# Experts with their third products inside the next expert's first one, and a second input projection begun during the first output projection

## The chip, the cores and the metric

The kernel runs on one core of one Trainium2 chip. The core has five engines with instruction queues of their own, which run in order: TensorE (PE, with its weight loads shown as PEld), VectorE (DVE), ScalarE (ACT), GpSimd (POOL) and SyncE (SP), on which most DMAs are issued. They wait for one another by semaphores. The metric is the device time of one execution in microseconds.

## The reference

Two model blocks stand one after the other, with 2,048 tokens of 1,024 columns. The first is a layer with attention and a Fourier branch. The second has latent attention beside a gated recurrence (mLSTM), then a mixture of experts, then a gated embedding and a last norm. All in 32-bit floats; where a product needs the precision, the kernel splits a factor into a rounded high part and a low remainder (`hi`, `lo`) and adds three products. The parts that the change touches:

```python
# end of the first block
h = h + jnp.einsum('ble,ed->bld', mixed, w_out[i]); h = rmsnorm(h, final_g)
# second block: input projection
h = _rmsnorm(x, norm_mix_g[i])
c_q, c_kv, k_r, x_m, z, i_pre, f_pre = _split_in(h @ w_in[i])
q = (_rmsnorm(c_q, q_norm_g[i]) @ w_uq[i]).reshape(B, S, MLA_HEADS, NOPE_D + ROPE_D)
kv = (_rmsnorm(c_kv, kv_norm_g[i]) @ w_ukv[i]).reshape(B, S, MLA_HEADS, NOPE_D + V_D)
q_rope, k_rope = _apply_rope(q[..., NOPE_D:], cos, sin), _apply_rope(k_r, cos, sin)
...
# 32 experts, each token goes to two of them
def expert(args):
    xb, e = args
    return (jax.nn.silu(xb @ w_g[e]) * (xb @ w_u[e])) @ w_d[e]
```

## The kernel before

The program is a chain of phases. `phase_d` is the first output projection: 16 tiles of 128 tokens, three products of 512 columns for each pair of factors. `phase_e` is the second input projection, in eight groups of 256 tokens: `prep` reads a group's rows, norms them, transposes them on PE (L878) and splits them into `uhi` and `ulo`; a product with 424 columns of the weights (`th`, `tl`) gives the latents and gates, then one with 1,024 columns (`fh`, `fl`). These weights are read from memory and split on ACT and DVE (L76, L77) at the phase's start. `phase_f` makes queries, keys and values of the latents in four groups of 512 tokens: for each group it loads the rope tables (`cs`, `kr`), and three results (keys, queries, values) pass through a staging tile `o` with two buffers, copied by ACT and DVE in turn (`put`, L1081 and L1083) and stored from SP.

`phase_k` walks over the 32 experts; a step is called a block here. An expert has one tile of up to 128 tokens and, where more tokens came to it, a second one of 64 (`second`; here 16 of the 32, experts 0 to 6, 16, 17, 19, 21 to 25 and 28). In block x PE runs, in this order: two transposes of `sg`, the last expert's gated hidden rows (`out_a`, L2115); for a second tile `hidden2` (L2095, L2096); the first and second products of expert x (`hidden`, eight k steps of three products into `g`, with transposes of the next expert's rows between them, L2061, L2076, and of the second tile's `t` after the seventh step, L2136); `out_b`, the third products of expert x−1 into `py`; and `out2_b`, those of the second tile. Beside that the next weights are split: `raw` to `gh` on ACT and `gl` on DVE, `KW` = 2 slices of 256 columns (512) at a time, and `sd` to `dh` on ACT and `dl` on POOL, 512 columns at a time; DVE and ACT also do `sg` (L2090, L2091), the second tile's `t` (L2105, L2106, L2108, L2109), the splits of transposed rows (`xl`, `al`, `a`) and the copies of `py` to `y` (L2130, L2149). POOL gathers the rows of a later expert (L2049) and adds results to memory (L2052). All these helpers are L73 (ACT) and L74 (the other engine) of `split`. The tile framework sets the order on each engine and the waits; the two forms of a block stand in the two branches of an If.

Of the kernel before, what the change touches and what calls it, by code (L numbers as in the profile page):

```python
# [792 lines left out]
def phase_d(e):  # L793
# [5 lines left out]
    def post(wk, sm, pt, gb):  # L799
        def run(t, r, y):  # L800
            if t == 16:
                return
# [10 lines left out]

def phase_e(e, then):

# [10 lines left out]
    with ExitStack() as st:  # L826
# [3 lines left out]
        ut = pool("e_ut", 2)  # L830
        wk = pool("e_wk", 2)
        wt = pool("e_wt", 1)
        sm = pool("e_sm", 4)
        wp = pool("e_w", 1)
        pt = pool("e_pt", 2, space=PSUM)
        pm = pool("e_pm", 3, space=PSUM)
# [14 lines left out]
        fh, fl = load_split(e, wp, ld, w_in, 1024, 1024, "f", gcol, 416)  # L851
# [3 lines left out]
        taps = cst.tile([128, 4, 5], F32, name="taps")  # L855
        for k in range(4):
            nc.sync.dma_start(taps[:, :, k], d["conv_w_2"][0, k].rearrange("(h p) -> p h", p=128))
        nc.sync.dma_start(taps[:, :, 4], d["conv_b_2"][0].rearrange("(h p) -> p h", p=128))
        xms = [cst.tile([128, 4, 3 + GB], F32, name=f"xm{i}") for i in range(2)]
        nc.gpsimd.memset(xms[0][:, :, :3], 0.0)  # L860

        def prep(g):
            hi = ut.tile([128, 8, GB], F32R, name="uhi")
            lo = ut.tile([128, 8, GB], F32R, name="ulo")
            for i in range(GB // 128):
# [4 lines left out]
                junk = wk.tile([128, D], BF, name="junk", bufs=1)  # L870
# [11 lines left out]
        prep(0)  # L882
        pend = []
# [16 lines left out]
        for g in range(NG):  # L900
# [5 lines left out]
            for i in range(GB // 128):  # L906
# [6 lines left out]
                junk = wk.tile([128, D], BF, name="junk", bufs=1)  # L913
# [80 lines left out]
def phase_f(e, then):  # L994
# [16 lines left out]
    with ExitStack() as st:  # L1011
# [38 lines left out]
        yield  # L1050
        gates(e, pool)
        xp.append(pool("f_x1", 1))
        ld = pool("f_ld", 2)
        wk = pool("f_wk", 2)
        ps = pool("f_ps", 6, space=PSUM)
        e.stage = ld
        for g in range(S // GB):
            c = slice(g * GB, (g + 1) * GB)
            cs = ld.tile([128, 2, GB], F32, name="cs")
            for i, T in enumerate((CT, ST)):  # L1060
                nc.sync.dma_start(cs[:, i, :], bass.AP(tensor=T.tensor, offset=T.offset + g * GB, ap=[[0, 4], [S, 32], [1, GB]]))
            kr = ld.tile([64, GB], F32, name="kr")
            nc.sync.dma_start(kr, KRW[:, c])
# [7 lines left out]
            nc.sync.dma_start(KRT[:, c], ko[:, 0])  # L1071
# [7 lines left out]
            def put(o, p, i):  # L1079
                if i % 2:  # L1080
                    nc.scalar.activation(o, p, AF.Copy)  # L1081
                else:
                    nc.vector.tensor_copy(o, p)  # L1083
# [13 lines left out]
            nc.sync.dma_start(rows(QRT), r)  # L1097
            e.beside(then)
# [884 lines left out]
KW = 2  # L1983


def phase_k(e, last):
# [11 lines left out]
    with ExitStack() as st:  # L1998
# [13 lines left out]
        py = pool("k_py", 3, space=PSUM)  # L2012
# [26 lines left out]
        def split_down(w, s, x):  # L2039
            for k in range(2):  # L2040
                for i in range(2):
                    c = slice(i * 512, (i + 1) * 512)
                    split(e, w[0][:, k, c], w[1][:, k, c], s[:, 2 * k + i], eng=nc.gpsimd)
                    if k == i == 1 and x < 32:
                        load_down(x, s)
                    yield
# [37 lines left out]
        def hidden(w, x, sg, beside=lambda k: None):  # L2084

            g = pg.tile([128, 512], F32, name="g1")
# [33 lines left out]
        def out_b(w, a, dst):  # L2120
            y = op.tile([128, D], F32, name="y")
            for j in range(2):
                yp = py.tile([128, 512], F32, name="py")
                c = slice(j * 512, (j + 1) * 512)
                for k in range(2):
                    mm3(e, yp, (a[0][:, k], a[1][:, k]), (w[0][:, k, c], w[1][:, k, c]), k == 0, k == 1)
# [100 lines left out]
        def block(x, second):  # L2227
# [4 lines left out]
            if x:  # L2232
                a = out_a(SG[x - 1])
            parts(2)
            if second:
                sg2 = hidden2(W[x % 2], x2, x % 2)
                parts(2)
            a2 = []

            def beside(k):  # L2240
# [4 lines left out]
                if k == OUT2 and second:  # L2245
                    a2.append(out2_a(sg2))
# [4 lines left out]
                parts(1)  # L2251

            hidden(W[x % 2], X[x], SG[x], beside)
            if x:
                out_b(WD[(x - 1) % 2], a, e.dst[:, 0, x - 1:x])
            parts(16)
            if x < 31:
                all_of(split_down(WD[y], RD[y], x + 3))
            if second:
                out2_b(WD[x % 2], a2[0], e.dst[0:64, 1, x:x + 1])  # L2260
# [17 lines left out]
TURN, OUT2, TURN2 = (0, 2), 6, (4, 5)  # L2278
# [111 lines left out]
def body(e):  # L2390
    tc = e.tc
    with tc.tile_pool(name="consts", bufs=1) as cp:
# [9 lines left out]
        for _ in phase_d(e):  # L2402
            pass
# [52 lines left out]
```

## Time and profile before

| | us |
|---|---|
| runs (three) | 3589.45, 3594.97, 3596.04; median 3594.97 |
| profiled execution | 3607.51 |
| its span, mean granted clock | 3605.8, 0.966 |
| PE, PEld busy | 3364.2 (93%), 2611.3 (72%) |
| DVE, ACT, POOL busy | 2448.4 (68%), 2052.4 (57%), 696.2 (19%) |
| read from and written to memory | 333.81 MB, 135.24 MB |

The profiled execution is some 12.5 us longer than the median of the runs. By the trace `phase_d` runs from about 1357 us of the span to 1537, `phase_e` to 1827, `phase_f` to 1931, and the experts from 2892 to about 3380. A share of busy time is a mean over stages with different limits, so the stages are read one by one.

### The profile page before, as it was taken

What the parts mean: (1) busy time and instruction counts of PE and PEld (TensorE: products, weight loads), DVE (VectorE), ACT (ScalarE), POOL (GpSimd) and SP (SyncE); (2) the same over time, 40 slices, a digit from 0 to 9 for tenths busy, and PEclk for the clock granted to TensorE, in tenths of its full rate; (3) what the DMA queues carried; (4) which work ended last, traced back from release to release, by engine and by line L of the source; (5) the groups of instructions that cost most, each with busy time, mean ns of one, the idle gap of its engine ahead of it and who ended that gap; (6) DMA issues with size and microseconds to landing.
All of it is one profiled execution on the core that took longest, in us unless ns stands there. A gap on an engine that the chain in (4) does not pass through costs nothing. (4 is left out here: it accounts for less than half of the span.)

```text
span 3605.8 us, 48799 instructions
## 1 busy us (share of the span) xinstructions
PE 3364.2 (93%) x16556; PEld 2611.3 (72%) x16557; DVE 2448.4 (68%) x4612; ACT 2052.4 (57%) x3660; POOL 696.2 (19%) x729
## 2 busy tenths in 40 slices
PE   8999999999999999989986889989999989899798
PEld 6787766666666657789975667777788766677587
DVE  5835667888888854464365777877856568878554
ACT  4442357887777872253223777877833367677433
POOL 0000000000000010000032333332200046665332
PEclk9999999999999999999997999999999989899899
DMA  5333322111112035353247433322355678888753
GB/s 157 102 121 101 97 70 72 46 31 50 43 32 57 11 91 179 121 153 109 74 148 173 93 77 74 81 69 59 88 174 157 222 260 305 319 301 307 256 189 132
DMA packets 313432, 468.82 MB, mean 130 GB/s; under 512 B 66263, under 2 KB 201192, under 8 KB 304864
## 3 DMA queue, kind: packets, MB, share of 16 engines
q1 hardware_dynamic: 293622, 404.26, 36.9%
q0 software_dynamic: 19520, 60.97, 4.6%
q8 instruction: 148, 2.42, 0.3%
q14 instruction: 142, 1.16, 0.1%
HBM read 333.81 MB, written 135.24 MB: 130 GB/s over the span
## 5 line engine op out<-in xcount | busy, mean ns | idle before, releaser
L588 DVE TENSOR_TENSOR pl<-pe,ph 128x1024 fp32r<-128x1024 f32 (+1 forms) x272 | 340.6, 1253 | 89.0 <-ACT ph L581 87.7
L519 DVE TENSOR_REDUCE mx<-pmx 128x1 f32<-128x512 f32 x512 | 344.2, 684 | 82.9 <-PE pmx L518 76.5
L579 ACT ACTIVATE pe<-ps 128x1024 f32<-128x1024 f32 (+1 forms) x272 | 278.5, 1025 | 146.2 <-PE ps L577 135.9
L581 ACT ACTIVATE ph<-pe 128x1024 fp32r<-128x1024 f32 (+1 forms) x272 | 287.4, 1058 | 7.4
L74 DVE TENSOR_TENSOR gl<-raw,gh 128x512 fp32r<-128x512 f32 x256 | 235.2, 960 | 15.0 <-ACT gh L73 12.6
L576 PE MATMUL ps<-t,kh 128*128 128x512 f32 (+1 forms) x544 | 239.0, 439 | 0.5 <-ACT pe L579 0.5
L1280 DVE TENSOR_TENSOR pl<-pe,ph 128x512 fp32r<-128x512 f32 (+1 forms) x320 | 210.7, 662 | 40.5 <-ACT ph L1273 38.0
L577 PE MATMUL ps<-t,kl 65*128 65x512 f32 (+1 forms) x544 | 222.3, 409 | 0.0
L602 PE MATMUL acc<-ph,vh 128*65 128x512 f32 (+1 forms) x544 | 217.1, 399 | 0.0
L604 PE MATMUL acc<-pl,vh 128*65 128x512 f32 (+1 forms) x544 | 214.9, 395 | 0.0
L603 PE MATMUL acc<-ph,vl 128*65 128x512 f32 (+1 forms) x544 | 214.7, 395 | 0.0
L518 PE MATMUL pmx<-kh,t 128*128 128x512 f32 x512 | 207.1, 410 | 1.9 <-DVE mx L519 1.1
L1244 DVE TENSOR_REDUCE mx<-pmx 128x1 f32<-128x512 f32 (+2 forms) x320 | 190.7, 598 | 13.0 <-PE pmx L1243 12.6
L1271 ACT ACTIVATE pe<-ps 128x512 f32<-128x512 f32 (+1 forms) x320 | 166.9, 524 | 43.5 <-PE ps L1269 40.5
L74 POOL TENSOR_TENSOR dl<-sd,dh 128x512 fp32r<-128x512 f32 x128 | 172.8, 1371 | 71.6 <-ACT dh L73 69.2
L1273 ACT ACTIVATE ph<-pe 128x512 fp32r<-128x512 f32 (+1 forms) x320 | 179.5, 564 | 6.5
L1267 PE MATMUL ps<-t,kh 113*128 113x512 f32 (+1 forms) x320 | 138.0, 431 | 38.8 <-ACT pe L1271 29.8
L73 ACT ACTIVATE gh<-raw 128x512 fp32r<-128x512 f32 x256 | 143.4, 625 | 12.4 <-PE p L85 9.4
L83 PE MATMUL pm<-uhi,fh 128*128 128x256 f32 x512 | 145.3, 285 | 3.7 <-ACT fh L76 2.0
L84 PE MATMUL pm<-ulo,fh 128*128 128x256 f32 x512 | 143.6, 282 | 0.0
L85 PE MATMUL pm<-uhi,fl 128*128 128x256 f32 x512 | 143.2, 283 | 0.3 <-DVE fl L77 0.3
L788 DVE TENSOR_TENSOR y<-p,xt 128x1024 f32<-128x1024 f32 x32 | 39.2, 1224 | 152.9 <-PE p L85 151.2
(539 smaller groups left out, 9672.9 us busy)
## 6 DMA issues: line engine op xcount, KB each, us to landing
raw<-in_w_gate_e SPq DMA_DIRECT2D x32, 1024.0 KB
raw<-in_w_up_e SPq DMA_DIRECT2D x32, 1024.0 KB
sd<-in_w_down_e SPq DMA_DIRECT2D x32, 1024.0 KB
ws<-in_w_in SPq DMA_DIRECT2D x80, 256.0 KB
xt<-in_x SPq DMA_DIRECT2D x32, 512.0 KB
scr_X<-y SPq DMA_DIRECT2D x32, 512.0 KB
xt<-scr_X SPq DMA_DIRECT2D x32, 512.0 KB
yy<-scr_Y POOLq DMA_DIRECT2D x32, 512.0 KB, 5.0
```

Of the source, the lines that this page charges most:

```text
L74: (eng or nc.vector).tensor_tensor(lo, src, f32(hi), op=ALU.subtract)
L518: nc.tensor.matmul(p, t1[:, i * 128:(i + 1) * 128], kh[:, j * 512:(j + 1) * 512], start=True, stop=True)
L519: nc.vector.reduce_max(mx[:, i, j:j + 1], p, axis=AX.X)
L576: nc.tensor.matmul(p[:n, c], kh[:, k0:k0 + n], t1[:, c], start=True, stop=False)
L577: nc.tensor.matmul(p[:n, c], kl[:, k0:k0 + n], t2[:, c], start=False, stop=True)
L579: nc.scalar.activation(pe[:n], p[:n], AF.Exp, scale=0.125)
L581: nc.scalar.activation(ph[:n], pe[:n], AF.Copy)
L588: nc.vector.tensor_tensor(pl[:n], pe[:n], f32(ph[:n]), op=ALU.subtract)
L602: nc.tensor.matmul(A[u][j], vh[:n, i, :65], ph[:n, c], start=i == 0, stop=False)
L603: nc.tensor.matmul(A[u][j], vl[:n, i, :65], ph[:n, c], start=False, stop=False)
L604: nc.tensor.matmul(A[u][j], vh[:n, i, :65], pl[:n, c], start=False, stop=i == 16)
L1280: nc.vector.tensor_tensor(pl[:, c0:], pe[:, c0:], f32(ph[:, c0:]), op=ALU.subtract)
```

## The change

- `phase_e` begins inside `phase_d`: its constants, the 424 columns of weights, and group 0's rows are made beside `phase_d`'s last tiles (`NEXT`); the 1,024 columns and the rest come after it. Group buffers lie in two pools for that.
- `phase_f` reads the rope tables once, whole (18 DMAs), ahead of `gates`, and not per group; three staging buffers in place of two; of four copies out of PSUM ACT does three and DVE one, where each did two; the store of `ko` stands behind that of `r`.
- In the experts the third products (`out_b`, `out2_b`) stand after the sixth of the eight k steps of the next `hidden`, and their transposes after the fourth; `out_b` does its four products with `ah` ahead of its two with `al`. `g` has two PSUM buffers, `py` two in place of three. `KW` is 4, so that `gh` and `gl` are made 1,024 columns at a time; so are `dh` and `dl`.

The core of the diff:

```diff
-def phase_d(e):
+def phase_d(e, then):
...
     def post(wk, sm, pt, gb):
         def run(t, r, y):
+            if t == NEXT:
+                e.beside(then)
             if t == 16:
...
+NEXT = 13
...
 def phase_e(e, then):
...
-        ut = pool("e_ut", 2)
-        wk = pool("e_wk", 2)
+        ut = [pool("e_u0", 1)]
         wt = pool("e_wt", 1)
         sm = pool("e_sm", 4)
-        wp = pool("e_w", 1)
         pt = pool("e_pt", 2, space=PSUM)
-        pm = pool("e_pm", 3, space=PSUM)
...
             split(e, th[:, k], tl[:, k], ws[:, :NT], gcol[:, k:k + 1])
-        fh, fl = load_split(e, wp, ld, w_in, 1024, 1024, "f", gcol, 416)
...
         def prep(g):
-            hi = ut.tile([128, 8, GB], F32R, name="uhi")
-            lo = ut.tile([128, 8, GB], F32R, name="ulo")
+            hi = ut[g % 2].tile([128, 8, GB], F32R, name="uhi")
+            lo = ut[g % 2].tile([128, 8, GB], F32R, name="ulo")
...
         prep(0)
+        yield
+        wp = pool("e_w", 1)
+        ut.append(pool("e_u1", 1))
+        wk = pool("e_wk", 2)
+        pm = pool("e_pm", 3, space=PSUM)
+        fh, fl = load_split(e, wp, ld, w_in, 1024, 1024, "f", gcol, 416)
+        taps = wp.tile([128, 4, 5], F32, name="taps")
...
         yield
+        wt = pool("f_t", 1)
+        cst = wt.tile([128, 2, S], F32, name="cst")
+        krw = wt.tile([64, S], F32, name="krw")
+        for c in (slice(0, GB), slice(GB, S)):
+            for r in range(4):
+                for i, T in enumerate((CT, ST)):
+                    nc.sync.dma_start(cst[r * 32:(r + 1) * 32, i, c], T[:, c])
+            nc.sync.dma_start(krw[:, c], KRW[:, c])
         gates(e, pool)
         xp.append(pool("f_x1", 1))
         ld = pool("f_ld", 2)
-        wk = pool("f_wk", 2)
+        wk = pool("f_wk", 3)
         ps = pool("f_ps", 6, space=PSUM)
         e.stage = ld
         for g in range(S // GB):
             c = slice(g * GB, (g + 1) * GB)
-            cs = ld.tile([128, 2, GB], F32, name="cs")
-            for i, T in enumerate((CT, ST)):
-                nc.sync.dma_start(cs[:, i, :], bass.AP(tensor=T.tensor, offset=T.offset + g * GB, ap=[[0, 4], [S, 32], [1, GB]]))
-            kr = ld.tile([64, GB], F32, name="kr")
-            nc.sync.dma_start(kr, KRW[:, c])
+            cs, kr = cst[:, :, c], krw[:, c]
             xh, xl = X.pop(g)
...
@@ -1068,7 +1082,6 @@
             nc.gpsimd.tensor_tensor(ko[:, 0], kr[0:32], cs[0:32, 0], op=ALU.mult)
             nc.vector.tensor_mul(ko[:, 1], kr[32:64], cs[32:64, 1])
             nc.gpsimd.tensor_tensor(ko[:, 0], ko[:, 0], ko[:, 1], op=ALU.add)
-            nc.sync.dma_start(KRT[:, c], ko[:, 0])
...
             def put(o, p, i):
-                if i % 2:
+                if i:
                     nc.scalar.activation(o, p, AF.Copy)
                 else:
                     nc.vector.tensor_copy(o, p)
...
             nc.sync.dma_start(rows(QRT), r)
+            nc.sync.dma_start(KRT[:, c], ko[:, 0])
             e.beside(then)
             o = wk.tile([128, 4, GB], F32, name="o")
...
-KW = 2
+KW = 4
...
-        py = pool("k_py", 3, space=PSUM)
+        py = pool("k_py", 2, space=PSUM)
...
         def split_down(w, s, x):
             for k in range(2):
-                for i in range(2):
-                    c = slice(i * 512, (i + 1) * 512)
-                    split(e, w[0][:, k, c], w[1][:, k, c], s[:, 2 * k + i], eng=nc.gpsimd)
-                    if k == i == 1 and x < 32:
-                        load_down(x, s)
-                    yield
+                raw = s[:, 2 * k:2 * k + 2].rearrange("p a c -> p (a c)")
+                split(e, w[0][:, k], w[1][:, k], raw, eng=nc.gpsimd)
+                if k == 1 and x < 32:
+                    load_down(x, s)
+                yield
...
-            g = pg.tile([128, 512], F32, name="g1")
+            g = pg.tile([128, 512], F32, name="g1", bufs=2)
             for k in range(8):
...
             for j in range(2):
                 yp = py.tile([128, 512], F32, name="py")
                 c = slice(j * 512, (j + 1) * 512)
-                for k in range(2):
-                    mm3(e, yp, (a[0][:, k], a[1][:, k]), (w[0][:, k, c], w[1][:, k, c]), k == 0, k == 1)
+                terms = [(0, k, h) for k in range(2) for h in range(2)] + [(1, k, 0) for k in range(2)]
+                for n, (q, k, h) in enumerate(terms):
+                    nc.tensor.matmul(yp, a[q][:, k], w[h][:, k, c], start=n == 0, stop=n == 5)
...
             y = (x + 1) % 2
             steps = split_in(W[y], RG[y], x + 3) if x < 31 else iter(())
             parts = lambda n: [next(steps, None) for _ in range(n)]
-            if x:
-                a = out_a(SG[x - 1])
-            parts(2)
+            parts(1)
             if second:
                 sg2 = hidden2(W[x % 2], x2, x % 2)
-                parts(2)
-            a2 = []
+                parts(1)
+            a, a2 = [], []
             def beside(k):
                 if k in TURN and x < 31:
                     turn1(XR[(x + 1) % 2], X[x + 1], (TURN.index(k),))
                     if k == TURN[1]:
                         rows(x + 3)
-                if k == OUT2 and second:
-                    a2.append(out2_a(sg2))
                 if k in TURN2 and x % 2 == 1 and x < 31:
                     turn2(xr2, x2, (TURN2.index(k),))
                     if k == TURN2[1]:
                         rows2(x // 2 + 2)
-                parts(1)
+                if k == OUT and x:
+                    a.extend(out_a(SG[x - 1]))
+                if k == OUT and second:
+                    a2.append(out2_a(sg2))
+                if k == MID:
+                    if x:
+                        out_b(WD[(x - 1) % 2], a, e.dst[:, 0, x - 1:x])
+                    if second:
+                        out2_b(WD[x % 2], a2[0], e.dst[0:64, 1, x:x + 1])
+                if k % 2:
+                    parts(1)
             hidden(W[x % 2], X[x], SG[x], beside)
-            if x:
-                out_b(WD[(x - 1) % 2], a, e.dst[:, 0, x - 1:x])
-            parts(16)
+            parts(8)
             if x < 31:
                 all_of(split_down(WD[y], RD[y], x + 3))
-            if second:
-                out2_b(WD[x % 2], a2[0], e.dst[0:64, 1, x:x + 1])
             if x == 31:
                 out_b(WD[x % 2], out_a(SG[x]), e.dst[:, 0, x:x + 1])
...
-TURN, OUT2, TURN2 = (0, 2), 6, (4, 5)
+OUT, MID, TURN, TURN2 = 3, 5, (0, 2), (1, 4)
...
         e.flip()
         for _ in attention:
             pass
-        for _ in phase_d(e):
-            pass
-        e.flip()
         with ExitStack() as st:
             route = phase_j(e, st)
             first = embed(e, range(0, LATE), "right")
             out = phase_i(e, route, first)
             latent = phase_g(e, out)
             heads = phase_f(e, latent)
-            phase_e(e, heads)
+            second = phase_e(e, heads)
+            for _ in phase_d(e, second):
+                pass
+            e.flip()
+            for _ in second:
+                pass
             for rest in (heads, latent, out):
```

How the order moves is shown at three places. POOL, one block with a second tile (`dl` are the low parts of the down weights, the two L2052 or L2065 the additions of the first and of the second tile's result to memory). Before:

```order
L2049 DMA xr_28504<-scr_HF,tok 128x1024
L74 TENSOR_TENSOR dl_28449<-sd_28451,dh_28448 128x512 x3
L2052 DMA scr_Y<-y,dst 4096x1024
L74 TENSOR_TENSOR dl_28449<-sd_28451,dh_28448 128x512
L2052 DMA scr_Y<-y_30535,dst 4096x1024
```

Now:

```order
L2062 DMA xr_28500<-scr_HF,tok 128x1024
L2065 DMA scr_Y<-y,dst 4096x1024
L74 TENSOR_TENSOR dl_28457<-sd_28459,dh_28456 128x1024 x2
L2065 DMA scr_Y<-y_30362,dst 4096x1024
```

Three of four pieces of `dl` stood ahead of the addition of `y`; now both pieces, twice as wide, stand behind it.

DVE, one block with a second tile (`gl` are the low parts of the gate and up weights, `t` the second tile's gated rows, `xl` and `al` low parts of transposed rows). Before:

```order
L74 TENSOR_TENSOR gl_28445<-raw_28429,gh_28444 128x2x256
L74 TENSOR_TENSOR al<-pt,ah 128x256
L74 TENSOR_TENSOR gl_28445<-raw_28429,gh_28444 128x2x256 x6
L2106 TENSOR_TENSOR t_34775<-t_34775,g_34758 64x512
L74 TENSOR_TENSOR gl_28445<-raw_28429,gh_28444 128x2x256
L2109 TENSOR_TENSOR t_34775<-t_34775 64x256
L74 TENSOR_TENSOR xl<-pt,xh 128x512 x2
L74 TENSOR_TENSOR a_34834<-pt,a_34834 128x2x64
L2091 TENSOR_TENSOR sg<-sg,g_34785 128x256
L2130 COPY y<-py 128x512
L2149 TENSOR_TENSOR y_34871<-y_34871,py 64x512 x2
```

Now (a block that also has the row transposes of an odd expert, `x`):

```order
L74 TENSOR_TENSOR gl_28451<-raw_28433,gh_28450 128x4x256 x4
L2119 TENSOR_TENSOR t_34960<-t_34960,g_34943 64x512
L74 TENSOR_TENSOR xl<-pt,xh 128x512
L2122 TENSOR_TENSOR t_34960<-t_34960 64x256
L74 TENSOR_TENSOR x_28498<-pt,x_28498 128x8x64
L74 TENSOR_TENSOR xl<-pt,xh 128x512
L74 TENSOR_TENSOR al<-pt,ah 128x256
L74 TENSOR_TENSOR a_35015<-pt,a_35015 128x2x64
L74 TENSOR_TENSOR x_28498<-pt,x_28498 128x8x64
L2145 COPY y<-py 128x512
L2164 TENSOR_TENSOR y_35055<-y_35055,py 64x512 x2
L2104 TENSOR_TENSOR sg<-sg,g_34968 128x256
```

All four `gl` now stand ahead of `t`, and `sg` behind the copies of `y`.

ACT, from `phase_d`'s last norms on (L805 or L807 is the norm of a tile of `phase_d`, L871 or L868 that of a tile of `phase_e`). Before:

```order
L871 ACTIVATE junk,ss<-xt 128x1024 x2
L805 ACTIVATE junk,ss<-y 128x1024
L73 ACTIVATE uhi<-pt 128x4x128
L102 ACTIVATE rs_r<-ss 128x1
L73 ACTIVATE uhi<-pt 128x4x128 x3
L871 ACTIVATE junk,ss<-xt 128x1024
L76 ACTIVATE th<-ws,gcol 128x424 x3
L871 ACTIVATE junk,ss<-xt 128x1024
```

Now:

```order
L807 ACTIVATE junk,ss<-y 128x1024
L102 ACTIVATE rs_r<-ss 128x1
L73 ACTIVATE uhi<-pt 128x4x128 x2
L807 ACTIVATE junk,ss<-y 128x1024
L73 ACTIVATE uhi<-pt 128x4x128
L102 ACTIVATE rs_r<-ss 128x1
L73 ACTIVATE uhi<-pt 128x4x128
L76 ACTIVATE fh<-ws,gcol 128x512 x3
```

The eight splits of `th` have gone from here to the first tiles of `phase_d`, and those of `fh` come at once.

## Rows read from the trace of the kernel before

**Rows 1.** Busy times by stretch: length, PE, PEld, DVE, ACT, POOL (instructions), clock, DMA share, GB/s.

```profile
1357.00:1540.00 183.00, 174.88 (x756) 143.58 (x756) 80.88 (x160) 48.07 (x83) 1.67 (x3) 0.96 0.47 150
1860.00:1940.00 80.00, 52.39 (x198) 38.91 (x197) 42.85 (x80) 17.22 (x32) 15.74 (x20) 0.87 0.69 194
3080.00:3170.00 90.00, 78.91 (x363) 61.77 (x362) 73.35 (x96) 63.50 (x124) 56.26 (x45) 0.92 0.84 311
```

**Rows 2.** PE's waits, 1480 to 1620: releaser, total, times, longest.

```profile
PE pt L878 <- DVE ss L91: 2.9, 1, 2.9
PE pm L83 <- ACT th L76: 2.9, 2, 2.6
PE pm L83 <- ACT fh L76: 2.0, 2, 1.2
```

**Rows 3.** ACT in order of time at the start of `phase_e`: start, length, instruction, idle before.

```profile
1551.49 0.72 ACT L76 ACTIVATE fh<-ws,gcol 128x512 fp32r<-128x512 f32 x1 [0.35 <-DMA ws<-in_w_in]
...
1578.79 1.36 ACT L76 ACTIVATE fh<-ws,gcol 128x512 fp32r<-128x512 f32 x2 [1.02 <-DMA ws<-in_w_in]
```

**Rows 4.** PE's waits, 1827 to 1945.

```profile
PE p L83 <- ACT o L1081: 13.8, 4, 7.2
...
PE p L83 <- DVE t L1095: 3.5, 3, 1.9
```

**Rows 5.** Groups by line, 1827 to 1931: busy, mean ns, idle before and its releasers.

```profile
L1083 DVE COPY o<-p 128x512 f32<-128x512 f32 x24 | 15.8, 680 | 16.6 <-DMA scr_QNT<-o 12.1 <-DMA scr_KNT<-o 3.8 <-PE p L85 0.7
```

**Rows 6.** Groups by line in the experts, 2907 to 3376.

```profile
L74 DVE TENSOR_TENSOR gl<-raw,gh 128x512 fp32r<-128x512 f32 x240 | 220.3, 959 | 11.5 <-ACT gh L73 9.1 <-ACT ah L73 1.5
L74 POOL TENSOR_TENSOR dl<-sd,dh 128x512 fp32r<-128x512 f32 x122 | 163.8, 1363 | 69.6 <-ACT dh L73 69.2
...
L2115 PE MATMUL pt<-ident,sg 128*128 128x128 f32 x64 | 13.9, 302 | 31.7 <-DVE sg L2091 21.6 <-DVE y L2149 10.1
```

**Rows 7.** PE in order of time: starts of blocks (L2115), and `t`'s transposes in block 22.

```profile
3093.90 0.66 PE L2115 MATMUL pt<-ident,sg 128*128 128x128 f32 x2 [4.51 <-DVE sg L2091]
...
3120.91 0.66 PE L2115 MATMUL pt<-ident,sg 128*128 128x128 f32 x2 [4.51 <-DVE sg L2091]
...
3168.19 0.41 PE L2115 MATMUL pt<-ident,sg 128*128 128x128 f32 x2 [0.58 <-DVE y L2149]
...
3177.69 0.41 PE L2115 MATMUL pt<-ident,sg 128*128 128x128 f32 x2
...
3224.43 0.41 PE L2115 MATMUL pt<-ident,sg 128*128 128x128 f32 x2 [0.57 <-DVE y L2149]
...
3234.28 0.33 PE L2136 MATMUL pt<-ident,t 64*128 64x64 f32 x2
...
3240.68 0.41 PE L2115 MATMUL pt<-ident,sg 128*128 128x128 f32 x2 [0.57 <-DVE y L2149]
...
3257.73 0.41 PE L2115 MATMUL pt<-ident,sg 128*128 128x128 f32 x2 [0.58 <-DVE y L2149]
```

**Rows 8.** DVE in order of time around the start of block 22.

```profile
3222.07 0.69 DVE L2130 COPY y<-py 128x512 f32<-128x512 f32 x1 [1.90 <-PE py L85]
...
3225.47 2.25 DVE L74 TENSOR_TENSOR gl<-raw,gh 128x512 fp32r<-128x512 f32 x1 [0.27 <-ACT gh L73]
...
3227.97 3.68 DVE L74 TENSOR_TENSOR gl<-raw,gh 128x512 fp32r<-128x512 f32 x6
3231.59 0.67 DVE L2106 TENSOR_TENSOR t<-t,g 64x512 f32<-64x512 f32 x1
...
3232.78 0.41 DVE L2109 TENSOR_TENSOR t<-t 64x256 f32<-64x256 f32 x1
```

**Rows 9.** POOL in the same stretch.

```profile
3220.87 3.78 POOL L74 TENSOR_TENSOR dl<-sd,dh 128x512 fp32r<-128x512 f32 x3 [2.22 <-ACT dh L73]
3224.82 1.00 POOL L2052 DMA_INDIRECT scr_Y<-y,dst  x1 [0.17 <-issue]
3225.85 1.31 POOL L74 TENSOR_TENSOR dl<-sd,dh 128x512 fp32r<-128x512 f32 x1
```

**Rows 10.** Groups by line over the whole span: differences of 1,024 columns.

```profile
L2377 POOL TENSOR_TENSOR sg<-sg,x 128x1024 f32<-128x1024 f32 x16 | 38.1, 2381 | 48.1 <-DVE sg L2376 48.1
...
L74 DVE TENSOR_TENSOR ml<-mf,mh 128x1024 fp32r<-128x1024 f32 x32 | 38.8, 1216 | 8.3 <-DMA scr_MIX<-o 5.1 <-ACT mh L73 3.1
```

More of the change, by code (lines that the diff above doesn't have):

```diff
@@ L854, in phase_e @@
         NG = S // GB
[L855 to L860, printed above, removed]
         def prep(g):
-            hi = ut.tile([128, 8, GB], F32R, name="uhi")
-            lo = ut.tile([128, 8, GB], F32R, name="ulo")
+            hi = ut[g % 2].tile([128, 8, GB], F32R, name="uhi")
+            lo = ut[g % 2].tile([128, 8, GB], F32R, name="ulo")
             for i in range(GB // 128):
@@ L869, in prep @@
                 ss = sm.tile([128, 1], F32, name="ss")
-                junk = wk.tile([128, D], BF, name="junk", bufs=1)
+                junk = ld.tile([128, D], BF, name="junk", bufs=1)
                 nc.scalar.activation(junk, xt, AF.Square, accum_out=ss)
@@ L882, in phase_e @@
         prep(0)
+        yield
[5 more added lines that the diff above has]
+        taps = wp.tile([128, 4, 5], F32, name="taps")
+        for k in range(4):
+            nc.sync.dma_start(taps[:, :, k], d["conv_w_2"][0, k].rearrange("(h p) -> p h", p=128))
+        nc.sync.dma_start(taps[:, :, 4], d["conv_b_2"][0].rearrange("(h p) -> p h", p=128))
+        xms = [wp.tile([128, 4, 3 + GB], F32, name=f"xm{i}") for i in range(2)]
+        nc.gpsimd.memset(xms[0][:, :, :3], 0.0)
         pend = []
@@ L912, in phase_e @@
                 ss = sm.tile([128, 2], F32, name="ss2")
-                junk = wk.tile([128, D], BF, name="junk", bufs=1)
+                junk = ld.tile([128, D], BF, name="junk", bufs=1)
                 nc.scalar.activation(junk[:, :256], p[:, :256], AF.Square, accum_out=ss[:, 0:1])
```

## The prediction, made before the changed kernel ran

> **What bounds the kernel now.** I read the table of stretches first [rows 1], since the change touches three stages with different limits. In `phase_d` PE is busy 174.88 of 183 us, in 756 products, so 0.231 us a product of 512 columns; that stage is PE's. In 1860 to 1940 PE is busy only 52.39 of 80 us and no other engine is busier: there is waiting. Among the experts PE is busy 78.91 of 90, DVE 73.35, the DMA engines 0.84 of the time: several things are close. Then I asked what PE waited for. At the start of `phase_e` it waits for the norm's factor, for `th` and for `fh` [rows 2], and the splits of `fh` run from 1551.49 to 1580.15 while ACT waits for weights [rows 3]. In `phase_f` it waits 13.8 us for ACT's copies into `o` [rows 4], and DVE's copies into the same `o` wait for the store of the queries, 12.1 us, and of the keys, 3.8 [rows 5]. Among the experts the wait on the path is that of `out_a`'s transposes, 31.7 us in all [rows 6]: 21.6 for `sg`, mostly in blocks 8 to 15, and 10.1 for the copies of the block before, 0.57 in each block with a second tile.
>
> The last view is the order of time on DVE and POOL [rows 8, 9]. In block 22 a `gl` that would take about 0.6 us is there for 2.25 us, while POOL finishes an addition and then runs a `dl` of 1.31 us; it ends 0.56 after that `dl`. A mean of 959 ns for 240 `gl` [rows 6], against 3.68/6 = 0.613 for the six undisturbed ones behind it [rows 8], says that this is common: the two operations, both with two inputs in on-chip memory, are not done at once. The copies of `y` out of PSUM run beside `dl` undisturbed. That decides the prediction.
>
> **phase_e.** The splits of `th`, the first norms and group 0's transposes move into `phase_d`, whose ACT is busy 48 of 183 us and DVE 81, so they cost nothing there, save the 16 transposes, which only change place on PE. What goes at the boundary is 2.9 + 2.9 + 2.0 = 7.8 us of waits [rows 2] and a few us of slow products behind them. What is late next is `fh`: it needs memory that `phase_d` uses, so its splits start after the last store of `phase_d`, near 1541 by my estimate against 1551.49, and last as long as before, 28.7 us [rows 3]. The end of the weights moves by about 10.5 us. I take −10, between −4 (if the first loads wait longer) and −16.
>
> **phase_f.** Three buffers `o` for three uses a group take the wait for the stores away where the store is under one group old; whole tables take the small loads out of the groups. But SP stays in order, and the waits of `gates` for its own small stores stand ahead of the same stores of `o`. ACT does three copies of four instead of two, at a busy share of 17 of 80 us [rows 1]; that is hidden. At most 13.8 + 3.5 and some 4 us of loads go [rows 4], 21 us; at worst the 2 MB of tables ahead of `gates` cost 3 us. I take −8, near the half of rows 4, because the stores themselves are not shorter.
>
> **The experts.** What goes is the 0.57 us in front of a block and the wait for `sg`, since a second `g` lets PE begin at once. What comes is told by the order: on POOL both `dl` now stand behind the addition of `y`, on DVE all four `gl` ahead of `t`, and PE's transposes of `t` stand three k steps earlier.
>
> Block 22 worked out, from its start. PE came to `t`'s transposes 9.85 us in [rows 7]; three k steps fewer, 9 × 0.231 = 2.08, make it 7.8. When is `t` ready? Behind the end of `out_b` PE still has two k steps and `out2_b`, 14 × 0.231 = 3.2 us, to the block's end. In that time: a copy of `y`, 0.25 + 0.69 [rows 8], the addition, 0.2 + 1.00 [rows 9], then two `dl` of 1,024 columns. None is in the trace; POOL's other difference of that size, from on-chip memory, takes 2.381 [rows 10], and twice 1.26 is 2.5, so 2.38 each. Sum 2.15 + 4.76 = 6.9, so the second `dl` ends 3.7 us into the next block. The first `gl` there, ready at about 1.6, is held until then. Four `gl` at 1.2 (DVE's own difference of 1,024 columns is 1.216 [rows 10]) end at 8.5, `t`'s product at 9.1, its second one, 0.5 later, at 10.0, with both lengths as in [rows 8]. PE waits 10.0 − 7.8 = 2.2 us, less the 0.57 gone: +1.6 us a block. A block of an odd expert has two more transposed pieces in the same queue, +1.8.
>
> [...]
>
> [...]
>
> A block without a second tile behind one with it (18, 20, 26; 9.50 us from 3168.19 to 3177.69 [rows 7]): PE wants `al` for the last products of the first half of `out_b` 6.1 us in (six k steps, the transposes, four products); `al` comes behind three `gl`, two `xl` and itself, 3.7 + 3.6 + 1.7 = 9.0. So +2.9 − 0.57 = +2.3. In the run of blocks 8 to 15 (27.0 us a pair from 3093.90 to 3120.91 [rows 7]) the chain closes on itself: copy and addition 2.15, `dl` 2.38, `gl` 1.2, `dl` 2.38, two `gl` 2.4, `xl`, `xl`, `al` 1.7, and eight products after it 1.85: 14.1 us against 13.5, +0.6 a block.
>
> Sum: five even blocks of 16.2 us (2, 4, 6, 22, 24) × 1.6 and five odd ones of 17.05 (3, 5, 17, 23, 25) × 1.8 make 17; the six other blocks with a second tile, whose neighbours differ, at half of 1.7 make 5; 18, 20, 26 make 7; 7, 27, 29, 30 at half of 2.3 make 4.6; the run 4.8. Together +38. Bounds: all blocks in full and some clock lost to the new waits, +55; nothing held, as below, −28.
>
> Profiled execution: 3607.5 − 10 − 8 + 38 = 3627.5. It lay 12.5 above the median of the runs, so **3615 us**.
>
> **The rivals.** *The holds do not add up* (`dl` comes earlier, or the lock is not taken so). Then `gl` ends at 1.6 + 4.8 = 6.4, `t` is ready at 7.9, PE waits 0.1, and a block with a second tile gains about 0.4, 16 of them 6; the seven single ones gain 0.57, 4; in the run the 4.5 us a pair [rows 7] could go down to what DMA allows, 0.84 × 27.0 = 22.7, so 18 in four pairs. −28 − 18 = −46: 3549 if in full, 3570 with half of it. For: the addition may be given back by an earlier `out_b`. Against: rows 8 and 9.
>
> *phase_f opens up and the experts lose less.* With F at −21 and the experts at half, +19: −12, 3583; with F at −12, about 3592 to 3598. For: `o`'s waits have one cause [rows 4, 5]. Against: SP's order is kept.
>
> *The experts lose in full*, with PE's clock falling in the run, as it does by its gaps now (0.92 [rows 1]): +55 − 18 = +37, 3632, and up to 3649 if E and F give only −4 and +3. It decides once PE's waits within a block pass the 4.5 us of today.
>
> **Chances.** The forecast with the third rival 0.58, the first rival 0.25, the second 0.17. Two runs of this kernel can be told apart by about 0.2%, 7 us. Slower by more than that: 0.58; within: 0.11, out of the second rival and the forecast's edge; faster: 0.31. Cases of both signs hold most of the chance, so the forecast's own range is 3600 to 3645, and the whole range, which has to take in the half of the first rival, 3560 to 3646.
>
> **What would show it.** In the trace after: PE's waits at the transposes of `t` (L2151) of about 2 us in every block with a second tile, by DVE; the first `gl` of a block 2 to 3 us long, ending just after the second `dl`, which ends 3 to 4 us into the block; blocks of 17.8 and 18.9 us. No wait in front of a block. The last `fh` split some 10 us earlier against the end of `phase_d`. I am wrong if `dl` of 1,024 columns ends within its own block, or blocks with a second tile come out under 16.2 us.

## The result, and the profile after

The changed kernel takes 3675.39 us (median of four runs, 3664.17 to 3683.18), the kernel before 3592.21. The ratio is 1.0221, 95% interval 1.0201 to 1.0241: slower, as forecast, but by 83 us and not 23; the time lies above the range.

| stage, by PE's products in the two traces | before | after | difference |
|---|---|---|---|
| up to the last product of `phase_d` | 1529.2 | 1528.1 | −1.1 |
| from there to the last product of `phase_e` | 297.9 | 288.4 | −9.5 |
| to the first scores of the latent attention (`phase_f`) | 113.6 | 103.7 | −9.9 |
| to its last scores | 677.0 | 666.3 | −10.7 |
| to the first product of an expert | 274.8 | 279.1 | +4.3 |
| to the last third product | 481.0 | 577.8 | +96.8 |
| to the end of PE's work | 219.8 | 220.7 | +0.9 |

So the experts lose 96.8 us and all the rest gains 26. The stretch of the experts in the table of stretches of the changed kernel (columns as in [rows 1]):

```profile
2865.50:3443.30 577.80, 472.17 (x2000) 358.30 (x2001) 362.90 (x392) 312.25 (x459) 266.14 (x155) 0.89 0.64 241
```

The same stretch of before:

```profile
2892.40:3373.40 481.00, 433.48 (x2000) 330.89 (x2000) 368.00 (x520) 336.72 (x650) 276.83 (x219) 0.95 0.79 291
```

The number of products is that of before, 2,000. DMA is down to 0.64, so memory is not the limit. The granted clock is 0.89, and it was 0.95. What PE waited for in the changed kernel's experts, whole list of the groups over 0.9 us (releaser, total, times, longest):

```profile
PE pt L2128 <- DVE xl L74: 43.8, 14, 4.7
PE pt L2151 <- DVE t L2122: 26.2, 8, 4.6
PE py L2141 <- DVE al L74: 22.1, 8, 3.8
PE py L2141 <- ACT ah L73: 7.7, 9, 1.1
PE pt L2151 <- DVE x L74: 4.9, 8, 0.6
PE g L2108 <- ACT dh L73: 1.1, 1, 1.1
PE pt L2128 <- DVE sg L2104: 0.9, 1, 0.9
```

The waits in front of a block are gone ([rows 6] had 31.7 us of them; 0.9 us is left, after the last block). In their place stand 106.7 us of waits inside the blocks, nearly all on DVE: for `t`, for `al`, and, the largest, at `out_a`'s transposes (L2128), which wait for a `pt` tile that DVE's `xl` has still to read. All of PE's waits in the experts before were 47.5 us.

DVE and POOL in a block with a second tile, in order of time (start, length, instruction, idle before), the rows that answer to [rows 8, 9]. DVE:

```profile
3303.72 0.69 DVE L2145 COPY y<-py 128x512 f32<-128x512 f32 x1 [2.05 <-PE py L2141]
...
3309.17 6.34 DVE L74 TENSOR_TENSOR gl<-raw,gh 128x1024 fp32r<-128x1024 f32 x4 [1.27 <-ACT gh L73]
3315.43 0.67 DVE L2119 TENSOR_TENSOR t<-t,g 64x512 f32<-64x512 f32 x1
3316.03 0.67 DVE L74 TENSOR_TENSOR xl<-pt,xh 128x512 fp32r<-128x512 f32 x1
3316.63 0.40 DVE L2122 TENSOR_TENSOR t<-t 64x256 f32<-64x256 f32 x1
```

POOL:

```profile
3305.20 1.01 POOL L2065 DMA_INDIRECT scr_Y<-y,dst  x1 [3.72 <-ACT dh L73]
3306.21 4.80 POOL L74 TENSOR_TENSOR dl<-sd,dh 128x1024 fp32r<-128x1024 f32 x2
```

PE in the same block:

```profile
3314.26 0.38 PE L2128 MATMUL pt<-ident,sg 128*128 128x128 f32 x2
3317.18 0.31 PE L2151 MATMUL pt<-ident,t 64*128 64x64 f32 x2 [2.54 <-DVE t L2122]
3317.42 0.72 PE L83 MATMUL g<-gh,xh 128*128 128x512 f32 x1
3317.93 0.63 PE L84 MATMUL g<-gl,xh 128*128 128x512 f32 x1
3318.36 0.63 PE L85 MATMUL g<-gh,xl 128*128 128x512 f32 x1
```

The two `dl` end at 3311.01, 7.29 us after the copy of `y` began (in block 22 of before 5.09 [rows 8, 9]). The four `gl` begin at 3309.17 and take 6.34, where four take 4.63 with no `dl` on POOL (e3, below). The first of them alone:

```profile
3309.17 2.93 DVE L74 TENSOR_TENSOR gl<-raw,gh 128x1024 fp32r<-128x1024 f32 x1 [1.27 <-ACT gh L73]
```

It ends 1.09 us behind the second `dl`, about the length of one `gl`, so it is held until that is done. PE waits 2.54 us for `t`, and behind that wait its products come 0.43 us apart and not 0.23: the granted clock is 0.52 from 3317.4 to 3320.5.

By the two rows of stretches, PE's idle time in the experts grew from 481.0 − 433.48 = 47.5 us to 577.8 − 472.17 = 105.6, by 58.1. Its busy time, for the same 2,000 products, grew from 433.48 to 472.17, by 38.7. The first part is the new waits; the second is put down to the lower clock, since the products are the same. Together they are the 96.8.

The hold itself is not new. All `gl` of the changed kernel's experts, by line:

```profile
L74 DVE TENSOR_TENSOR gl<-raw,gh 128x1024 fp32r<-128x1024 f32 x124 | 221.7, 1827 | 34.1 <-ACT gh L73 34.1
```

They take 221.7 us, and 145.8 where nothing holds them (e3, below); before, 240 took 220.3 [rows 6], where 240 of 0.613 would take 147. So the `gl` were held about as long in all, and what is new is that PE asks earlier for what stands behind them on DVE: `t`, `xl` and `al` (e10 shows the same from the other side).

### The profile page after: what moved, and what is told of

The parts are those of the page before. It is cut to its first block, busy times and chain, and to the rows that moved or that the text cites. A ratio compares the mean times of both kernels' runs of the same rounds, so it can differ in the third digit from the quotient of the medians.

```text
span 3676.7 us, 48251 instructions
## 1 busy us (share of the span) xinstructions
PE 3391.6 (92%) x16556; PEld 2630.5 (72%) x16557; DVE 2438.2 (66%) x4472; ACT 2034.5 (55%) x3480; POOL 685.8 (19%) x665
## 5 line engine op out<-in xcount | busy, mean ns | idle before, releaser
L74 DVE TENSOR_TENSOR gl<-raw,gh 128x1024 fp32r<-128x1024 f32 x128 | 226.6, 1808 | 35.7 <-ACT gh L73 35.6
L1258 DVE TENSOR_REDUCE mx<-pmx 128x1 f32<-128x512 f32 (+2 forms) x320 | 190.7, 598 | 11.8 <-PE pmx L1257 11.7
L1281 PE MATMUL ps<-t,kh 113*128 113x512 f32 (+1 forms) x320 | 136.6, 427 | 34.8 <-ACT pe L1285 27.4
L74 POOL TENSOR_TENSOR dl<-sd,dh 128x1024 fp32r<-128x1024 f32 x64 | 153.9, 2446 | 4.0 <-ACT dh L73 3.9
L73 ACT ACTIVATE gh<-raw 128x1024 fp32r<-128x1024 f32 x128 | 127.4, 1050 | 21.1 <-DVE sg L2104 10.5
L83 PE MATMUL pm<-whi,uhi 128*128 128x512 f32 (+1 forms) x384 | 138.6, 362 | 0.0
```

Of the source, the lines that this page charges most:

```text
L74: (eng or nc.vector).tensor_tensor(lo, src, f32(hi), op=ALU.subtract)
L83: t.matmul(out, a[0], b[0], start=start, stop=False)
```

## Experiments

Every run is given with its ratio to the kernel before on the same chip; before had medians of 3588.79, 3594.77 and 3597.49 us in the three sets of experiments, and the 3592.21 above in the set of the changed kernel. "Experts" is the time from the first product of an expert to the last third product in the profiled execution.

| run | median us | ratio, 95% interval | experts us |
|---|---|---|---|
| changed kernel | 3675.39 | 1.0221, 1.0201 to 1.0241 | 577.8 |
| e1 phases e, f alone | 3579.71 | 0.9971, 0.9953 to 0.9988 | 490.2 |
| e2 `dl` narrow | 3567.44 | 0.9937, 0.9915 to 0.9959 | 469.0 |
| e3 `dl` on DVE | 3562.36 | 0.9927, 0.9910 to 0.9944 | 458.8 |
| e4 `gl` narrow | 3685.28 | 1.0271, 1.0252 to 1.0291 | 587.8 |
| e5 `dl` wide, by output columns | 3613.85 | 1.0060, 1.0036 to 1.0083 | 512.8 |
| e6 `dl` narrow, over both halves | 3653.40 | 1.0159, 1.0128 to 1.0191 | 562.1 |
| e7 `t` later | 3648.55 | 1.0143, 1.0116 to 1.0169 | 543.9 |
| e8 e3 and e7 | 3564.94 | 0.9911, 0.9885 to 0.9936 | 461.6 |
| e9 experts alone | 3689.68 | 1.0273, 1.0246 to 1.0301 | 575.7 |
| e10 wide pieces alone | 3627.77 | 1.0093, 1.0063 to 1.0123 | 511.6 |
| e11 `dl` on DVE, by output columns | 3556.98 | 0.9907, 0.9880 to 0.9933 | 458.2 |
| e12 all pieces narrow | 3579.39 | 0.9957, 0.9943 to 0.9972 | 487.6 |

**e1 and e9: the two halves of the change.** e1 is the kernel before with the parts of the diff in `phase_d`, `phase_e`, `phase_f` and `body`; e9 is the kernel before with the rest:

```diff
-KW = 2
+KW = 4
 # and the diff's parts in phase_k alone
```

e1: 

> The changes in phase_e and phase_f alone, the experts as before. Theory (the experts alone lose, by some 97 us between their first product and the last third product): the time of the changed kernel less 97, so faster than before by 15 to 30 us, 3562 to 3577. Rival (part of the loss comes from another stage, moved there by what begins early): between 3600 and 3660.

e9: 

> The changes in the experts alone, phase_e and phase_f as before. Theory (the parts add up): before plus 97, less what one profile is off, 3675 to 3700; experts from first to last product 570 to 585 us, as in the changed kernel. Rival (the experts lose because something started in phase_e or phase_f stands in their way): under 3650.

e1 gains 0.29%, 10 us (4 to 17): clear, but less than the theory's range. Its trace has `phase_e` at 289.6 us and `phase_f` at 103.8, as in the changed kernel; its experts, unchanged code, took 9 us longer than in the profile of before. e9 loses the whole, 2.7% or 98 us, with experts of 575.7. The experts alone lose. e9 also has 666.5 us of scores in the latent attention with `phase_e` and `phase_f` as before, and e1 665.9 with the experts as before: neither half of the change is needed for the 10.7 us there, so I do not count them as the change's.

**e2: `dl` and `dh` in pieces of 512 again.** The rest of the change stays.

```diff
-                raw = s[:, 2 * k:2 * k + 2].rearrange("p a c -> p (a c)")
-                split(e, w[0][:, k], w[1][:, k], raw, eng=nc.gpsimd)
+                for i in range(2):
+                    c = slice(i * 512, (i + 1) * 512)
+                    split(e, w[0][:, k, c], w[1][:, k, c], s[:, 2 * k + i], eng=nc.gpsimd)
...
```

> The changed kernel, but with dl and dh in pieces of 512 columns as before; by the order three of the four dl then stand ahead of POOL's addition again. Theory (the two wide dl stand behind the addition, end 3.9 us into the next block and hold its first gl; PE's waits and the half clock after them follow from that): the last dl ends about 2.2 us into the block, the waits at t fall from 2.5 to about 0.8 us, the clock stays up in the blocks with a second tile, 3605 to 3630. Rival (the order on PE asks for t and sg too early, whatever POOL does): 3665 to 3685, waits as they are.

It took 3567, better than the theory asked for: this edit alone is worth 108 us, and the kernel beats the one before. Its POOL:

```profile
3205.69 3.81 POOL L74 TENSOR_TENSOR dl<-sd,dh 128x512 fp32r<-128x512 f32 x3 [4.46 <-ACT dh L73]
...
3210.66 1.32 POOL L74 TENSOR_TENSOR dl<-sd,dh 128x512 fp32r<-128x512 f32 x1
```

and its DVE:

```profile
3206.43 0.69 DVE L2146 COPY y<-py 128x512 f32<-128x512 f32 x1 [3.59 <-PE py L2142]
...
3211.83 4.65 DVE L74 TENSOR_TENSOR gl<-raw,gh 128x1024 fp32r<-128x1024 f32 x4 [1.17 <-ACT gh L73]
```

The first `dl` starts before the copy of `y`, since by the code its 512 columns are read by the first half of `out_b` alone; the last ends 5.55 us after the copy began, 0.15 into the first `gl`, and the four `gl` take 4.65. PE's waits in the experts:

```profile
PE pt L2129 <- DVE xl L74: 14.4, 11, 3.0
PE pt L2152 <- DVE t L2123: 11.0, 8, 4.2
PE py L2142 <- ACT ah L73: 6.2, 9, 1.0
PE pt L2152 <- DVE x L74: 4.9, 8, 0.6
PE py L2142 <- DVE al L74: 3.0, 5, 1.0
```

The three large waits, for `xl`, `t` and `al`, shrink together, 92 us to 28: the pieces of `dl` and `dh` were behind all of them. (e3, where `dh` stays wide, leaves 21.5 us, so it was `dl`.) The experts' stretch has the clock back:

```profile
2870.30:3339.30 469.00, 426.88 (x1999) 323.08 (x2000) 304.57 (x392) 318.24 (x522) 275.36 (x219) 0.98 0.79 296
```

POOL is busy longer than in the changed kernel, 275 against 266 us, and the time is 108 us shorter. POOL's load was not the matter.

**e3: `dl` on DVE.**

```diff
-                split(e, w[0][:, k], w[1][:, k], raw, eng=nc.gpsimd)
+                split(e, w[0][:, k], w[1][:, k], raw)
```

> The changed kernel, but dl is made by DVE, not by POOL, so that no dl can hold a gl. DVE has 2.4 us more to do in each block. Theory (holding): the first gl takes 1.2 us and not 2.9, the wait at t falls from 2.5 to about 1.5 us, which in the traces so far is too short to cost the clock; 3630 to 3650. Rival (DVE is simply too full in front of t, by its own work): waits at t grow to over 3 us and the time to 3690 or more.

It went past the theory's range, 3562. DVE, with 2.36 us of `dl` of its own in each block:

```profile
3225.25 0.69 DVE L2145 COPY y<-py 128x512 f32<-128x512 f32 x1 [2.05 <-PE py L2141]
3226.17 2.36 DVE L74 TENSOR_TENSOR dl<-sd,dh 128x1024 fp32r<-128x1024 f32 x2 [0.22 <-ACT dh L73]
...
3231.27 4.63 DVE L74 TENSOR_TENSOR gl<-raw,gh 128x1024 fp32r<-128x1024 f32 x4 [1.22 <-ACT gh L73]
```

Two wide `dl` take 4.80 us on POOL and 2.36 on DVE, and DVE has had idle time there. The last ends 3.28 us after the copy began. All 124 `gl` take 145.8 us here, 1.18 each, so none is held; 113 us of time are gone with the hold.

No run has `dl` on DVE in the old order. What the new order is worth beside that move is therefore not shown.

**e5 and e6: place against width.** e5 keeps the width of 1,024 and cuts by output columns; e6 has the width of 512, but each piece spans both halves:

```diff
 # e5
...
+                split(e, w[0][:, :, c], w[1][:, :, c], s[:, i::2], eng=nc.gpsimd)
 # e6
...
+                hi, lo = (w[h][:, k].rearrange("p (a c) -> p a c", a=2)[:, :, c] for h in range(2))
+                split(e, hi, lo, s[:, 2 * k:2 * k + 2, c], eng=nc.gpsimd)
```

e5: 

> The changed kernel, dl and dh still in two pieces of 1,024 columns a partition, but each piece is the same 512 output columns of both k slices, so that the first one needs only the first half of out_b to be done; by the order it stands ahead of POOL's addition. Theory (the place of dl, set by what a piece overwrites, decides, not its width): last dl ends about 2 us into the next block, 3560 to 3585. Rival (width: one long hold costs more than two short ones): half-way or more to the changed kernel, 3620 to 3680.

e6: 

> The changed kernel with four pieces of dl and dh of 512 columns, but each piece spans both halves of the output columns (256 of each), so that none can begin before both halves of out_b are done; by the order three pieces stand behind the addition. Theory (place): the last piece ends some 3.5 us into the next block, so 3640 to 3680, near the changed kernel. Rival (width): as the pieces of 512 by halves, 3560 to 3590, since a gl can come between short pieces.

e6 came as the theory has it, e5 as neither: 3614. Its edit did not bring the last `dl` to the place that the theory had: it ends 3.2 us into the next block, not about 2. So e5 does not decide between place and width. The rows of e5, POOL and DVE:

```profile
3243.30 2.39 POOL L74 TENSOR_TENSOR dl<-sd,dh 128x1024 fp32r<-128x1024 f32 x1 [2.57 <-ACT dh L73]
...
3246.89 2.42 POOL L74 TENSOR_TENSOR dl<-sd,dh 128x1024 fp32r<-128x1024 f32 x1
```

```profile
3242.98 0.69 DVE L2145 COPY y<-py 128x512 f32<-128x512 f32 x1 [2.05 <-PE py L2141]
...
3248.06 5.74 DVE L74 TENSOR_TENSOR gl<-raw,gh 128x1024 fp32r<-128x1024 f32 x4 [0.90 <-ACT gh L73]
```

and of e6:

```profile
3266.46 1.30 POOL L74 TENSOR_TENSOR dl<-sd,dh 128x512 fp32r<-128x512 f32 x1 [7.73 <-ACT dh L73]
...
3268.92 3.81 POOL L74 TENSOR_TENSOR dl<-sd,dh 128x512 fp32r<-128x512 f32 x3
```

```profile
3265.84 0.69 DVE L2147 COPY y<-py 128x512 f32<-128x512 f32 x1 [5.17 <-PE py L2143]
...
3271.83 5.41 DVE L74 TENSOR_TENSOR gl<-raw,gh 128x1024 fp32r<-128x1024 f32 x4 [1.77 <-ACT gh L73]
```

In e5 the first `dl` has to wait for a whole wide `dh`, so it starts 0.32 after the copy and not 0.74 before it. The time of these five kernels goes along with one number, the end of the last `dl` after the start of the copy of `y`, in a block with a second tile: 3.28 (e3), 5.55 (e2), 6.33 (e5), 6.89 (e6), 7.29 us (changed kernel), with medians of 3562, 3567, 3614, 3653, 3675 us. From 5.55 to 7.29 that is 108 us for 1.74, about 2 us a us in each of 31 blocks. It goes along as well with how long the `gl` are held: all of them take 145.8, 162.9, 188.4, 208.9 and 221.7 us. Neither number holds outside of these five: e7, below, ends its `dl` as late as the changed kernel and takes 27 us less, and e10 holds its `gl` longer and takes 48 us less. What counts as well is when PE asks for the results.

**e7 and e8: `t` asked for later.**

```diff
-                if k == OUT and second:
-                    a2.append(out2_a(sg2))
                 if k == MID:
                     if x:
                         out_b(WD[(x - 1) % 2], a, e.dst[:, 0, x - 1:x])
+                    if second:
+                        a2.append(out2_a(sg2))
+                if k == 7:
                     if second:
                         out2_b(WD[x % 2], a2[0], e.dst[0:64, 1, x:x + 1])
```

e7: 

> The changed kernel, wide dl on POOL, but t's transposes after the sixth k step and out2_b after the eighth, so PE asks for t 1.4 us later. Theory (waits of 2.5 us are followed by 3.4 us at half clock, shorter ones not): in even blocks with a second tile the wait falls to about 1.1 us and the half clock goes, 3.1 us a block, 3645 to 3660. Rival (the clock's level has another cause): 1.4 us a block alone, 3660 to 3668, half clock after the shorter wait too.

e8, with e3's edit: 

> dl on DVE as in the run before, and t's transposes and out2_b late as in the kernel beside it. Theory (what is left at t, 10.8 us in eight blocks, is a matter of when PE asks): 3548 to 3558. Rival (out2_b at the block's end makes its copies stand in front of the next sg and gl): 3562 to 3575.

e7 landed in the range, 27 us better than the changed kernel. In even blocks such as 22 and 24 PE no longer waits for `t`; it waits 0.93 to 0.97 us for `ah`, and these blocks run at clock 1.00 (all the experts at 0.92, in the changed kernel at 0.89). Such a block and the odd one behind it take 34.9 us, against 39.0 to 40.5 in the changed kernel (from the last product of one `hidden` to that of the next). Of PE's waits for `xl` and `al` 60 us are left. But that short waits leave the clock alone is not so: in e5 the products went from 0.23 to 0.43 us apart 1.8 us behind a wait of 1.58 us, while in the changed kernel the granted clock stayed at 1.00 (3297 to 3303) behind 1.90 and 0.62 us in one odd block. What decides is open. e8 landed in the rival's range, not clear of e3: PE's wait for `t` fell from 10.8 to 2.2 us, and 9.0 us for `a` and 5 more for `ah` came in its place.

**e4 and e12: the width of `gh` and `gl`.** `KW` is 2, with the smaller pieces spread over the k steps as before; e12 has e2's edit as well, so e12 is the new order of the blocks with all pieces narrow.

e4: 

> The changed kernel, but gh and gl in pieces of 512 columns as before; dl stays wide. Theory (dl's place and width decide): within 10 us of the changed kernel, 3665 to 3685, the first gl still held until the second dl ends. Rival (the four wide gh in a row on ACT make gl and t late): 3620 to 3650.

e12: 

> The changed kernel with all pieces (gh, gl, dh, dl) of 512 columns as before: the new order on PE and the PSUM tiles alone. Theory (the width of gl does not matter, that of dl does by its end): as with dl alone narrow, 3558 to 3572. Rival (wide gh and gl save fixed costs on ACT and DVE): 3575 to 3590.

e4 lies at the edge of the theory's range, slower than the changed kernel by 10 us in the medians and in the experts, and by 0.5%, 18 us, in the ratios. So wide `gh` and `gl` help a little there; they were not part of the loss. e12 lies in the rival's range, 3579, and not in the theory's. Against e2 its median is 12 us worse and its experts 18.6, but the intervals of the ratios overlap. What wide pieces save shows in the traces: a wide `gh` takes 1.05 us on ACT in the changed kernel, two narrow ones 1.25 in the kernel before; a wide `gl` 1.16 (e3), two narrow ones 1.23 by [rows 8].

**e10: wide pieces in the old order.**

```diff
-KW = 2
+KW = 4
 # and split_down in two pieces of 1,024
```

> The kernel before with pieces of 1,024 columns alone (gh, gl, dh, dl); order of the blocks on PE as before. Theory (a wide piece of dl overwrites both halves of a weight and so begins and ends later, and the time follows the end of the last dl): last dl ends about 6.9 us after the copy of y begins, 5.1 before; old order leaves it 2 us more room, so 3600 to 3640. Rival (wide pieces hurt with the new order alone): 3575 to 3595.

3628, as the theory has it: wide pieces hurt in the old order too, 31 us in the experts, where the new order, with `t` and `al` asked for earlier, makes it 97. All `gl` of the experts take 243.4 us here, more than the 221.7 of the changed kernel: the old order bears a longer hold at a third of the loss. With all pieces narrow the new order costs 6.6 us in the experts (e12), which two profiles of one code can differ by (e1), so most of the 97 comes from the two together.

**e11: `dl` on DVE, cut by output columns.** e5's cut without `eng=nc.gpsimd`.

> The changed kernel with dl on DVE and cut by output columns, so that its first piece needs the first half of out_b alone. Theory: both pieces are done about 1 us earlier than with dl on DVE cut by rows, wait at t from 1.4 to about 0.6 us, 3552 to 3560. Rival (sg and the copies now stand behind dl on DVE): 3562 or more.

3557, the best median, within the range; but the experts take 458.2 us as in e3 and the wait for `t` fell by 1.5 us in all only, so the theory's reason is not shown and the two cannot be told apart. e3, e8 and e11 all beat both kernels, by about 0.7 to 0.9% and 3%.

## Why the prediction was wrong, step by step

- *phase_e, −10.* Measured −9.5: right in size, by luck in part. PE's list has no wait for `th` left. But the splits of `fh` run from 1534.94 to 1561.88 and so end 18 us earlier, not 10.5, and PE's waits in the stage fell by 3 us alone, since it now waits longer for two other results (`ev`, `xm`). The rest, 6.6 us, is PE's busy time: the clock is 1.00 and not 0.98, and 16 transposes stand in `phase_d`.
- *phase_f, −8.* Measured −9.9 (with this code as before, e9 took 111.2 us and e10 111.5, so −7.5 to −9.9). The waits for `o` [rows 4] are 3.9 us instead of 13.8; a new one of 11.8, for the next group's `xh`, took back more than that and was not foreseen. All of PE's waits in the stage fell from 32.8 to 27.4, its busy time from 80.8 to 76.1. Right in size, but not by the way that was forecast.
- *The order on POOL and DVE; the first `gl` held until the second `dl` ends.* Right: it is done after the second `dl`, and the two take 4.80 (4.76 predicted).
- *PE's wait at `t`, 2.2 us.* Measured 2.54 to 2.58 in the five even blocks. Right. In odd ones 1.90 for `xl` and 0.62; about as predicted. In blocks 0, 16 and 28, put at half, it was 4.3 to 4.6.
- *The sum of the experts, +38.* This is the step that failed; measured +96.8. Three of its terms were wrong.
  - *The clock*, which the sum left out and only the upper bound had, "some clock lost to the new waits". It cost some 39 us. The third rival had it begin once the waits in a block pass 4.5 us; it came behind a single wait of 2.54. Four pairs of an even block and the odd one behind it (2 and 3, 4 and 5, 22 and 23, 24 and 25) took 33.3 us each before and were to lose 3.4; two took 39.0 and two 40.5.
  - *The run*, "14.1 us against 13.5, +0.6 a block". Measured 33.7 a pair from 3042.5 to 3076.2, +3.4 a block. PE, then DVE, in that pair:

```profile
3042.47 0.69 PE L2128 MATMUL pt<-ident,sg 128*128 128x128 f32 x2 [3.78 <-DVE xl L74]
...
3062.24 1.22 PE L2141 MATMUL py<-dh,al 128*128 128x512 f32 x2 [3.58 <-DVE al L74]
...
3076.19 0.69 PE L2128 MATMUL pt<-ident,sg 128*128 128x128 f32 x2 [3.53 <-DVE xl L74]
```

```profile
3032.31 0.69 DVE L2145 COPY y<-py 128x512 f32<-128x512 f32 x1 [2.74 <-PE py L2141]
...
3044.66 0.41 DVE L74 TENSOR_TENSOR al<-pt,ah 128x256 fp32r<-128x256 f32 x1
...
3050.02 0.69 DVE L2145 COPY y<-py 128x512 f32<-128x512 f32 x1 [2.18 <-PE py L2141]
...
3061.78 0.41 DVE L74 TENSOR_TENSOR al<-pt,ah 128x256 fp32r<-128x256 f32 x1
...
3066.07 0.69 DVE L2145 COPY y<-py 128x512 f32<-128x512 f32 x1 [2.75 <-PE py L2141]
```

  The chain was followed to `al` rightly (12.8 and 12.2 us after the copy, 12.0 by the sum), but behind it I put only the eight products that `al` feeds, 1.85. In the first block PE had been held earlier, at `out_a`'s transposes, which waited for `xl` on DVE; when `al` came, PE was in the second of the two k steps behind them and had all of `out_b` in front of it, at a granted clock of 0.72: 4.95 us from `al` to the next copy of `y`. There two results from one engine queue were counted as one wait. In the second block PE did wait for `al`, 3.58 us, as forecast, and the clock alone was missing: its eight products ran at a granted clock of 0.50, 3.88 us to the next copy.
  - *Blocks put at half.* 27 and 30 were to lose half of 2.3 each. They took 16.7 and 17.0 us and not 10.4 and 9.8, and so behave like the blocks of the run.
  - In the other direction, the last third products no longer wait 8.4 us for `ah`; that gain was not in the sum either.
- *The rivals.* The third, the full loss with the clock, named the mechanism, at 3632 to 3649, and fell short by 26 us or more. The second needed the experts at half and did not come. The first, that the holds do not add up (its "lock" is the hold read from [rows 8, 9], 2.25 us for a `gl` against 0.613), is refuted by the first `gl`, held until both `dl` are done, and by e3, where `dl` leaves POOL and nothing else changes.
- *Four `gl` at 1.2.* Right: without a hold they take 4.63 us (e3), 1.16 each; eight narrow ones would take 4.90 by [rows 8]. How much of e4's 10 to 18 us these 0.27 us a block make is not shown, since the narrow `gl` of e4 were also held longer (247.3 us for all).

## What to carry to other kernels

Before a piece of work is made larger, look at what it overwrites: a larger piece has to wait for the last reader of all of it, and here it began later by more than it saved (the first `dl` 3.2 us later than in e2 against the copy of `y`, and all pieces together 0.3 us shorter). Price a new wait of a few us on TensorE with the clock that may follow it (here 58 us of waits and 39 us of slower products), and follow each queue that feeds PE on its own: a tile that is not read back holds PE well before the value that one is looking at. When several waits grow at once, look for the one late operation that they share and take it away, here by moving `dl` to an engine with idle time.

## What the runs showed of the hardware that was not expected

- Two differences of 1,024 columns from on-chip memory took 4.80 us on POOL and 2.36 on DVE, and in e3 the move was a gain of 113 us although DVE was busier than POOL in the experts (363 against 266 us).
- A `gl` that waited did not get in between two `dl`. In the run of blocks of the changed kernel, POOL and then DVE (the last line is the first of the two `gl` alone):

```profile
3034.79 4.79 POOL L74 TENSOR_TENSOR dl<-sd,dh 128x1024 fp32r<-128x1024 f32 x2
```

```profile
3036.45 5.36 DVE L74 TENSOR_TENSOR gl<-raw,gh 128x1024 fp32r<-128x1024 f32 x2 [0.96 <-ACT gh L73]
3036.45 4.23 DVE L74 TENSOR_TENSOR gl<-raw,gh 128x1024 fp32r<-128x1024 f32 x1 [0.96 <-ACT gh L73]
```

  The first `gl` is there from 3036.45, the first `dl` ends halfway through, near 3037.2, and the second at 3039.58. The first `gl` ends 1.1 us behind that, at 3040.68, and the two at 3041.81. Of the changed kernel's `gl` 14 came like this, while one `dl` ran with another right behind it, and none got in between. Narrower `dl` alone do not change that: in e6 none of 23 did. In the kernel before, where the `gl` were narrow too, 17 of 18 did. What decides is open.
- The four `gl` without a hold took 4.63 to 4.65 us, 1.16 each, against twice 0.613 for six of half the width in [rows 8]: about 5% less.
